# Loading the pages of a paged cache: plain DMAs on the sync queue with the page number in a register, in place of indirect gathers on GpSimd

## The chip, the cores and the metric

The kernel runs on one NeuronCore of a Trainium2 chip. The metric is the time of the whole program on the device in microseconds (us): 1012.88 us is the median of three runs of the kernel before (1011.87 to 1016.22). A change below about 0.5% (5 us) can't be told from no change with this kernel. Engines are named as in the profile: PE (TensorE's matmuls), PEld (its weight loads), DVE (VectorE), ACT (ScalarE), POOL (GpSimd) and SP (SyncE, which here only issues DMAs).

## The reference: what is computed

One layer of a hybrid decoder for two groups that share all weights: a prompt of 512 positions and 8 samples with one new position each. Per layer:

```
x += W_out [ GatedDeltaNet heads (8 x 64) | NSA heads (8 x 64) ]( RMSNorm(x) @ W_in )
x += MemCrossAttn( RMSNorm(x), mem K/V )      (4 heads x 256, 256 memory tokens)
x += relu( RMSNorm(x) @ W_up )^2 @ W_down
```

and a final RMSNorm. The prompt has no past. Each sample has a past of 256 positions, which lies in a paged cache: `page_table[b, 0..1]` holds the numbers of two pages of 128 positions, out of 20 pages in all. For every sample the pages of its past are used three times: their compressed keys (`cmp_k`) and compressed values (`cmp_v`) go through a small MLP, and their selected keys and values (`slc_k`, `slc_v`) are attended to directly. So 16 pages are loaded four times, each time another 64 KB quarter of the page (128 rows of 512 bytes): 64 loads in all.

```
kv_all = jnp.concatenate([kv_past, kv_rows], axis=1)          # kv_past = pages[page_table]
k_cmp = compress_blocks(kv_all[:, :, 0], cmp_pe[0], cmp_w1[0], cmp_b1[0], cmp_w2[0])
v_cmp = compress_blocks(kv_all[:, :, 1], cmp_pe[1], cmp_w1[1], cmp_b1[1], cmp_w2[1])
```

## The kernel before

All activations are kept with features on the partitions. A weight panel of 128 output columns (`wraw`, 512 KB) is loaded by SP, split by ACT and DVE into a high and a low part (`whi`, `wlo`; `split`, L235 and L236), and multiplied in three matmuls for each of 8 pieces of the contraction (`mm3`, L194 by way of `mm`) with the two halves of the positions, 256 and 264 wide. The two buffers of `wraw` and of `whi`/`wlo` set how early a panel can be loaded.

`mixers` is the part that the change touches. It runs first a fixed sequence: the panels of the gates and of k0, k1, q0, q1 of the delta rule, the compressed keys `ck` (L500 stands behind it), then the panels k2, k3, q2, q3 with the compression MLP of the keys between them (`cmp_hidden(0)`). Behind that, `weave` lets five generators take turns by an estimate of the time on PE: `rule` (the delta rule: solve, then the chain over four chunks, `dn_chain`, whose step L888 to L928 needs the state of the step before), `nsa_samples`, `nsa_prompt` (the attention of the prompt), `fill` (the remaining panels of W_in and then `mem_kv`, the 16 panels `w_mk` and `w_mv` of the memory's keys and values, as filler for PE) and `mixed`. On top of this the framework orders the instructions of every engine with a simulated timeline (`TILE = dict(schedule_with_timeline_sim=True)`); so the order on each engine, and where a DMA stands in its queue, is decided there, not by the order of the source alone. Each queue works in that order: a DMA whose wait isn't met holds up all that stand behind it on the same queue.

Pages are loaded by `gather` (L517 to L520). It is called from two places. `cmp_gather(kind)` (L535) loads 16 quarters of pages into the tile G, for the keys (kind 0) after `ck`, for the values (kind 1) when the MLP of the keys has read G; G lies in the space of the tile x, so that the first burst waits for the last reader of x, an ACT square (L396). `nsa_samples` (L1273, L1276) loads the selected keys into the space of the tile qk0 and the selected values into the first half of the tile P; both belong to the delta rule and come free piece by piece when the matmuls of `dn_mats` and of the chain have read them. Before the change each of the 64 loads is an indirect DMA on POOL's queue, which takes its 128 row numbers from the tile `idx`, worked out by one DVE instruction from the page table:

```
self.nc.gpsimd.indirect_dma_start(
    out=out, out_offset=None, in_=self.I["pages"],
    in_offset=bass.IndirectOffsetOnAxis(ap=self.idx[:, k:k + 1], axis=0), element_offset=off)
```

In the profile these are `DMA_INDIRECT` instructions of L518. `cAQ` (L932) is a load of the chain's matrix from DRAM on SP's queue; it has one buffer, so that a load waits until PE has read the one before.

Of the kernel before, what the change touches and what calls it, by code (L numbers as in the profile page):

```python
# [10 lines left out]
I32 = mybir.dt.int32  # L11
AF = mybir.ActivationFunctionType
ALU = mybir.AluOpType
# [13 lines left out]
C_ID, C_TRI, C_UP, C_BLK, C_I64, C_CMPM, C_CMPA, C_HB, C_OWN, C_PP, C_CAU = (  # L27
    0, 128, 256, 384, 512, 576, 608, 640, 648, 664, 665)
# [153 lines left out]
class Build:  # L182
# [325 lines left out]
    def load_pages(self):  # L508
        nc, I, mp = self.nc, self.I, self.mp
        pg = mp.tile([128, 16], I32, name="pg")  # L510
        nc.sync.dma_start(pg[:], I["page_table"])
        self.idx = mp.tile([128, 16], I32, name="idx")
        nc.vector.tensor_scalar(self.idx[:], pg[:], 128.0, self.cst[:, C_PP:C_PP + 1], op0=ALU.mult, op1=ALU.add)
        self.w2 = mp.tile([128, 2, 64], F32, name="w2")
        nc.sync.dma_start(self.w2[:], I["w2"])

    def gather(self, out, k, off):  # L517
        self.nc.gpsimd.indirect_dma_start(  # L518
            out=out, out_offset=None, in_=self.I["pages"],
            in_offset=bass.IndirectOffsetOnAxis(ap=self.idx[:, k:k + 1], axis=0), element_offset=off)  # L520


    def cmp_tile(self, kind, h, ps):
# [1304 lines left out]
```

## Time and profile before

| what | before |
|---|---|
| median of 3 runs | 1012.88 us (1011.87 to 1016.22) |
| the profiled execution's own time | 1010.35 us |
| its span, first to last instruction | 1008.6 us |
| mean granted clock of PE | 0.98 |
| busy: PE, DVE, ACT, POOL | 953.5, 693.5, 483.8, 212.8 us |
| indirect DMAs on POOL (L518): into G, qk0, P | 32, 16, 16: 35.9, 17.5, 15.3 us busy |
| DMA moved | 123.78 MB, mean 123 GB/s |

The profile is of one execution. A row of the groups gives the line, the engine, the operation, what it writes and reads, how often, then its busy time and the mean of one in ns, then the idle time of the engine just before it and what ended that. `SPq` rows are SP's queue: the time beside them is that from the first to the last issue of the merged row, not of the transfer. In the chain of waits, "another core or an unknown queue" is a wait whose release the profile can't put down to an instruction, and "issue" is time in which the engine waited for nothing that the profile shows.

### The profile page before, as it was taken

To read this page: it belongs to the slowest core of one execution; us is meant where nothing else is said; L and a number is where in the kernel's file an instruction comes from. 1 tells how busy PE (TensorE), PEld (TensorE's weight loads), DVE (VectorE), ACT (ScalarE), POOL (GpSimd) and SP (SyncE) were. 2 spreads that over 40 slices of the span, in tenths; PEclk is the share of its full clock that TensorE was granted. 3 is DMA by queue.
4 is the path that set the end of the run, shared out by engine and by line. 5 is a ranking of instruction groups with operands and counts; after the bars stand their busy time and mean duration, and the time that the engine had idled before them with its cause. 6 is when DMAs were issued, how large, how long until landed. Compare 5 with 4: busy or idle time off the path is not lost.

```text
span 1008.6 us, 20477 instructions
## 1 busy us (share of the span) xinstructions
PE 953.5 (95%) x8160; PEld 877.5 (87%) x8160; DVE 693.5 (69%) x1406; ACT 483.8 (48%) x1041; POOL 212.8 (21%) x273
## 2 busy tenths in 40 slices
PE   6999798999968999999999999999999999999995
PEld 5988597798856886679998889999999999999995
DVE  6788349898734877865656558799766676666533
ACT  4675213158633635535444446567445544445331
POOL 2634615813074315202400002200000000000020
PEclk9999799999988999999999999999999999999998
DMA  7355243212011464344636634023323232323302
GB/s 272 115 176 162 96 143 126 72 67 75 24 40 51 146 221 178 133 173 157 251 141 240 228 129 161 2 84 126 109 92 105 95 105 85 116 84 108 123 12 85
DMA packets 49832, 123.78 MB, mean 123 GB/s; under 512 B 7608, under 2 KB 15480, under 8 KB 47016
## 3 DMA queue, kind: packets, MB, share of 16 engines
q1 hardware_dynamic: 45480, 109.10, 31.0%
q0 software_dynamic: 4256, 13.37, 3.7%
q8 instruction: 64, 1.05, 0.4%
q14 instruction: 32, 0.26, 0.1%
HBM read 111.06 MB, written 13.47 MB: 123 GB/s over the span
## 4 chain that ended last, share of the span: by engine, by line
PE 83%; DVE 9%; issue 2%; another core or an unknown queue 2%; DMA 1%; ACT 1%; POOL 0%; DVEq 0%; SPq 0%; ACTq 0%; POOLq 0%
PE ps_g L194 37%; PE ps_o L194 14%; PE ps_m L194 11%; PE ps_t L194 10%; PE ps_s L194 8%; PE ps_t L226 2%; DVE wlo L236 1%; PE ps_m L226 1%; DVE nb L806 1%; DVE x L1625 1%; DVE kp L1159 1%; DVE st L821 1%; DMA cAQ<-aqd 1%; DVE Xd L823 0%
## 5 line engine op out<-in xcount | busy, mean ns | idle before, releaser
L194 PE MATMUL ps_g<-xh,whi 128*128 128x264 f32 (+1 forms) x672 | 196.2, 293 | 3.4 <-ACT xh L235 1.1
L194 PE MATMUL ps_g<-xl,whi 128*128 128x264 f32 (+1 forms) x672 | 194.4, 290 | 2.4 <-DVE xl L236 1.5
L194 PE MATMUL ps_g<-xh,wlo 128*128 128x264 f32 (+1 forms) x672 | 193.2, 288 | 1.9 <-DVE wlo L236 1.5
L301 POOL TENSOR_TENSOR ssq<-ssq,sq 128x256 f32<-128x256 f32 (+2 forms) x47 | 44.4, 945 | 514.5 <-ACT sq L300 514.2
L194 PEld LDWEIGHTS ps_g<-xh,whi 128*128 128x128 f32 x672 | 128.9, 192 | 8.7 <-issue 4.3
L194 PEld LDWEIGHTS ps_g<-xh,wlo 128*128 128x128 f32 x672 | 128.5, 191 | 5.3 <-issue 2.7
L194 PEld LDWEIGHTS ps_g<-xl,whi 128*128 128x128 f32 x672 | 129.0, 192 | 3.8 <-DVE xl L236 1.6
L235 ACT CAST whi<-wraw 128x1024 fp32r<-128x1024 f32 (+1 forms) x67 | 69.6, 1040 | 103.1 <-PE ps_g L194 62.0
L235 ACT CAST wh<-wr 128x512 fp32r<-128x512 f32 x112 | 69.1, 623 | 66.7 <-PE ps_g L194 27.6
L236 DVE TENSOR_TENSOR wlo<-wraw,whi 128x1024 fp32r<-128x1024 f32 (+1 forms) x67 | 83.1, 1240 | 23.7 <-ACT whi L235 23.0
L236 DVE TENSOR_TENSOR wl<-wr,wh 128x512 fp32r<-128x512 f32 x112 | 76.4, 687 | 28.8 <-ACT wh L235 26.8
L194 PE MATMUL ps_g<-tyh,wl 128*128 128x260 f32 x256 | 72.3, 283 | 1.1 <-DVE wl L236 1.1
L194 PE MATMUL ps_g<-tyh,wh 128*128 128x260 f32 x256 | 72.6, 284 | 0.0
L194 PE MATMUL ps_g<-tyl,wh 128*128 128x260 f32 x256 | 72.5, 283 | 0.0
L194 PE MATMUL ps_o<-hh,wh 128*128 128x260 f32 x256 | 72.4, 283 | 0.0
L194 PE MATMUL ps_t<-hh,wh 128*128 128x260 f32 x256 | 72.4, 283 | 0.0
L194 PE MATMUL ps_t<-hh,wl 128*128 128x260 f32 x256 | 72.3, 283 | 0.0
L194 PE MATMUL ps_o<-hh,wl 128*128 128x260 f32 x256 | 72.3, 283 | 0.0
L194 PE MATMUL ps_o<-hl,wh 128*128 128x260 f32 x256 | 72.2, 282 | 0.0
L194 PE MATMUL ps_t<-hl,wh 128*128 128x260 f32 x256 | 72.1, 282 | 0.0
L235 ACT CAST wh<-ws 128x512 fp32r<-128x512 f32 x64 | 39.6, 619 | 48.0 <-PE ps_o L194 32.4
L236 DVE TENSOR_TENSOR wl<-ws,wh 128x512 fp32r<-128x512 f32 x64 | 43.8, 685 | 18.7 <-ACT wh L235 18.6
(470 smaller groups left out, 2616.3 us busy)
## 6 DMA issues: line engine op xcount, KB each, us to landing
wr<-in_w_up SPq DMA_DIRECT2D x64, 256.0 KB, 2.8
wr<-in_w_dn SPq DMA_DIRECT2D x64, 256.0 KB, 2.5
wraw<-in_w_in SPq DMA_DIRECT2D x26, 512.0 KB, 4.5
mK<-in_mkt SPq DMA_DIRECT2D x8, 1024.0 KB
mK<-in_mv SPq DMA_DIRECT2D x8, 1024.0 KB, 5.6
w<-in_w SPq DMA_DIRECT2D x8, 512.0 KB, 4.3
wraw<-in_w_mk SPq DMA_DIRECT2D x8, 512.0 KB, 3.2
wraw<-in_w_mv SPq DMA_DIRECT2D x8, 512.0 KB, 3.2
```

The source lines that it names most:

```text
L194: self.nc.tensor.matmul(out, lhsT, rhs, start=start, stop=stop, skip_group_check=True)
L226: self.nc.tensor.transpose(out, in_, self.ident[:k, :k])
L235: self.nc.scalar.copy(hi, x)
L236: self.nc.vector.tensor_tensor(lo, x, hi.bitcast(F32), op=ALU.subtract)
L301: nc.gpsimd.tensor_tensor(acc[:, :n], acc[:, :n], sq[:, :n], op=ALU.add)
L806: nc.vector.transpose(nb[s], P[s, :, s].rearrange("p c i -> p i c"))
L821: eng.tensor_tensor(tv, nb[:, j + 1:32, j].unsqueeze(2).to_broadcast([128, n, m]), x[:, j - c0, 0:m].unsqueeze(1).to_broadcast([128, n, m] ...
L1159: nc.vector.tensor_tensor(t[rows, 1, :], src, t[64 * g:64 * g + 64, 0, :].bitcast(F32), op=ALU.subtract)
L1625: nc.vector.scalar_tensor_tensor(x[:, i, :], ps, self.gain(4, i), x[:, i, :], op0=ALU.mult, op1=ALU.mult)
```

## The change

`load_pages` reads each of the 16 page numbers from the page table in SBUF into a register of SP, and `gather` becomes a plain DMA of SP's queue whose source begins at row 128 * page of the cache. The row numbers `idx` are no longer worked out. What is loaded, and where to, stays as it was.

```diff
-        self.idx = mp.tile([128, 16], I32, name="idx")
-        nc.vector.tensor_scalar(self.idx[:], pg[:], 128.0, self.cst[:, C_PP:C_PP + 1], op0=ALU.mult, op1=ALU.add)
+
+        n = I["pages"].shape[0] // 128
+        self.page = [nc.values_load(pg[0:1, k:k + 1], engines=[mybir.EngineType.SP], min_val=0, max_val=n - 1,
+                                    skip_runtime_bounds_check_because="entries of the page table are pages of the cache") for k in range(16)]
         self.w2 = mp.tile([128, 2, 64], F32, name="w2")
         nc.sync.dma_start(self.w2[:], I["w2"])
 
     def gather(self, out, k, off):
-        self.nc.gpsimd.indirect_dma_start(
-            out=out, out_offset=None, in_=self.I["pages"],
-            in_offset=bass.IndirectOffsetOnAxis(ap=self.idx[:, k:k + 1], axis=0), element_offset=off)
+        self.nc.sync.dma_start(out, self.I["pages"][bass.ds(self.page[k] * 128, 128), off:off + 128])
```

Since the simulated timeline orders each engine anew, here is where the loads come to stand. First SP's queue early in `mixers`, before the change: `wraw<-in_w_in` are panels of W_in (the fourth of the row `x4` is k2), `w<-in_w` the weights of the compression MLP, `cumd` and `P<-cumd` tables of the delta rule.

```order
L1282 DMA out_win_s<-in_win 8x4x16320
L243 DMA wraw<-in_w_in 128x1024 x4
L554 DMA w_962<-in_w 128x1024
L243 DMA wraw<-in_w_in 128x1024
L689 DMA cumd<-ct 32x128
L765 DMA P<-cumd 128x512 x8
```

and after the change:

```order
L1282 DMA out_win_s<-in_win 8x4x16320
L243 DMA wraw<-in_w_in 128x1024 x3
L514 TENSOR_LOAD pg
L520 ISA
L520 DMA G<-in_pages 128x128
...
L243 DMA wraw<-in_w_in 128x1024
L554 DMA w_1008<-in_w 128x1024
L243 DMA wraw<-in_w_in 128x1024
L689 DMA cumd<-ct 32x128
L765 DMA P<-cumd 128x512 x8
```

The three rows L514, L520, L520 stand there 16 times in a row: a load of a page number into a register, one instruction of register arithmetic, the DMA. All 16 stand ahead of the panel k2. The other 48 page loads have only the last two rows.

On POOL, the second burst into G and the loads into qk0 go, and what is left moves together (a piece of the difference):

```order
 L539 DMA G<-in_pe 128x32
-L518 DMA G<-in_pages,idx 128x128 x16
 L530 DMA out_kvp<-kv 128x520
-L518 DMA qk_214<-in_pages,idx 128x128 x2
 L604 DMA out_kvp<-nks 128x520
-L518 DMA qk_214<-in_pages,idx 128x128 x2
 L604 DMA out_kvp<-nkw 128x520
 L808 MEMSET Xs 128x1024
```

The third place is SP's queue where the chain of the delta rule starts; `wraw<-in_w_mk` are the panels of the memory's keys. Before:

```order
L243 DMA wraw<-in_w_in 128x1024 x12
L1635 DMA xm<-in_xm 128x1024 x2
L932 DMA cAQ<-aqd 128x1024 x2
L243 DMA wraw<-in_w_mk 128x1024 x5
L932 DMA cAQ<-aqd 128x1024
```

and after:

```order
L243 DMA wraw<-in_w_in 128x1024 x12
L1635 DMA xm<-in_xm 128x1024 x2
L932 DMA cAQ<-aqd 128x1024
L243 DMA wraw<-in_w_mk 128x1024
L520 ISA
L520 DMA qk_260<-in_pages 128x128
...
L520 DMA P<-in_pages 128x128
L243 DMA wraw<-in_w_mk 128x1024 x2
...
L932 DMA cAQ<-aqd 128x1024
L243 DMA wraw<-in_w_mk 128x1024 x4
```

The 24 page loads there (8 into qk0, 8 into P, and behind two panels another 8 into P) stand ahead of the second `cAQ`; the first panel of `w_mk` stands ahead of them all, and the second and third ahead of the last eight. Before, all five stood behind the second `cAQ`.

## The prediction

> **What bounds the kernel now.** First the page's busy times, the clock by slices, and the shares of the chain that ended last.
>
> ```profile
> span 1008.6 us, 20477 instructions
> ...
> PE 953.5 (95%) x8160; PEld 877.5 (87%) x8160; DVE 693.5 (69%) x1406; ACT 483.8 (48%) x1041; POOL 212.8 (21%) x273
> ...
> PEclk9999799999988999999999999999999999999998
> ...
> PE 83%; DVE 9%; issue 2%; another core or an unknown queue 2%; DMA 1%; ACT 1%; POOL 0%; DVEq 0%; SPq 0%; ACTq 0%; POOLq 0%
> ```
>
> PE sets the time: it is idle for 55 of 1008.6 us, and POOL, which issues the gathers, has no share in the chain. So the busy time that leaves POOL is worth nothing by itself. What the change can move is PE's 55 idle us, and the slices in which its clock falls (the fifth, the twelfth and the thirteenth of the 40). So I read PE's waits next: engine, line and releaser, then us in total, times, longest.
>
> ```profile
> PE ps_m L194 <- DVE S L928: 5.0, 1, 5.0
> PE ps_m L194 <- DVE kcz L576: 4.7, 1, 4.7
> ```
>
> Two long waits happened once each, behind DVE copies that are short. The timelines of PE and DVE show the first of them (start, duration, what; in brackets the idle time ahead and what ended it).
>
> ```profile
> 282.35 0.69 PE L194 MATMUL ps_m<-cvn,kt 128*64 128x64 f32 x16
> ...
> 289.57 0.80 PE L194 MATMUL ps_m<-S,qk 128*128 128x128 f32 x2 [5.03 <-DVE S L928]
> ```
> ```profile
> 288.64 0.88 DVE L928 COPY S<-ps_m 64x256 f32<-64x256 f32 x2 [5.15 <-remote]
> ```
>
> The copy of S needs only the matmuls on `cvn,kt`, which are recorded as done at 283.04. Yet DVE starts at 288.64, after 5.15 us of waiting for something that no instruction explains, and PE stands still behind it. The news of a finished matmul came over 5 us late. POOL's timeline says what ran meanwhile:
>
> ```profile
> 98.19 1.00 POOL L518 DMA_INDIRECT G<-in_pages,idx  x1 [0.30 <-issue]
> ...
> 117.39 0.94 POOL L518 DMA_INDIRECT G<-in_pages,idx  x1 [0.30 <-issue]
> ```
> ```profile
> 287.56 0.94 POOL L518 DMA_INDIRECT P<-in_pages,idx  x1 [0.30 <-issue]
> ```
>
> The eighth gather into P ends at 288.50, and 0.14 us later DVE is released. The last of the 16 gathers of the second burst ends at 118.33. The unexplained pieces of the chain of waits (start, us) fit both bursts:
>
> ```profile
> 106.61 4.39 another core or an unknown queue
> ...
> 111.45 3.76 another core or an unknown queue
> ...
> 115.93 2.11 another core or an unknown queue
> ```
> ```profile
> 283.49 5.13 another core or an unknown queue
> ...
> 296.69 3.92 another core or an unknown queue
> ```
>
> These five sum to 19.31 us, all between the first and last gather of a dense burst. That the gathers delay PE's signals is my reading of a coincidence in time; no row shows the mechanism. The windows give the size: from:to, length, busy us of PE, PEld, DVE, ACT, POOL, then clock, DMA share, GB/s.
>
> ```profile
> 105.00:125.00 20.00, 13.13 (x68) 9.99 (x66) 6.26 (x16) 4.48 (x8) 12.86 (x14) 0.74 0.22 68
> 250.00:275.00 25.00, 25.00 (x429) 21.39 (x428) 17.87 (x42) 15.85 (x44) 2.53 (x3) 1.00 0.09 31
> 282.00:325.00 43.00, 30.81 (x251) 23.81 (x250) 16.65 (x35) 14.11 (x39) 25.54 (x29) 0.80 0.14 47
> 325.00:350.00 25.00, 25.00 (x264) 20.13 (x263) 21.88 (x44) 16.93 (x45) 8.11 (x9) 1.00 0.45 148
> ```
>
> In the two bursts PE is idle for 6.87 and 12.19 us, at 0.74 and 0.80 of its clock; just before and behind the second it is never idle, at full clock. Bandwidth isn't short: the bursts move 68 and 47 GB/s, the quiet stretch behind 148. The clock is halved only behind each stall, and these windows cover the busy time at half clock:
>
> ```profile
> 119.00:125.00 6.00, 5.14 (x17) 3.81 (x17) 3.02 (x8) 2.42 (x4) 2.58 (x3) 0.51 0.20 61
> 289.00:296.00 7.00, 6.43 (x31) 5.43 (x32) 4.21 (x10) 1.83 (x5) 5.09 (x7) 0.53 0.13 40
> 303.00:306.00 3.00, 3.00 (x17) 2.03 (x16) 1.46 (x4) 1.16 (x3) 0.88 (x2) 0.53 0.06 22
> 316.00:323.00 7.00, 6.20 (x30) 4.70 (x32) 1.53 (x3) 1.60 (x5) 1.72 (x2) 0.51 0.22 84
> ```
>
> Busy time times the missing share of the clock: 5.14 x 0.49 = 2.5, 6.43 x 0.47 = 3.0, 3.00 x 0.47 = 1.4, 6.20 x 0.49 = 3.0; together 9.9 us. (The 0.26 and 0.20 of the whole windows would count idle time twice.)
>
> **The change part by part.** *Removed: the gathers.* Idle 6.87 + 12.19 = 19.1 us, and 9.9 us of half clock, are 29.0 us. The neighbouring windows put the natural idle time near nothing; I leave 1 us of it, so the gain is **28 us**. Bounds: nothing, if the stalls are not the gathers' doing; 29 and a few us more, if the panels issued earlier (below) fill idle time that I counted as natural. I take 28 because start and end of the stalls agree with the bursts to 0.2 us. POOL itself gets rid of 32 + 16 + 16 gathers,
>
> ```profile
> L518 POOL DMA_INDIRECT G<-in_pages,idx x32 | 35.9, 1123 | 9.7 <-issue 9.1 <-DMA G<-in_pages,idx 0.3 <-DVE cum L681 0.3
> ```
>
> some 36 us of busy time for G and, at the same mean, as much for the other 32, all off the path; the DVE instruction for `idx` goes too, a fraction of a us at the start, also off it.
>
> *Added: SP's first burst.* SP now carries 16 times a register load, register arithmetic and a DMA, ahead of panel k2. SP's queue today, the panel's landing, POOL's release of G and ACT's use of k2:
>
> ```profile
> 14.48 22.32 SPq L243 DMA_DIRECT2D wraw<-in_w_in  x4
> ...
> 53.62 4.86 SPq L765 DMA_DIRECT2D P<-cumd  x8
> ```
> ```profile
> wraw<-in_w_in SPq DMA_DIRECT2D x26, 512.0 KB, 4.5
> ```
> ```profile
> 30.10 0.73 POOL L539 DMA_DIRECT2D G<-in_pe  x1 [16.99 <-ACT sq L396]
> ```
> ```profile
> 53.94 1.05 ACT L235 CAST whi<-wraw 128x1024 fp32r<-128x1024 f32 x1 [2.54 <-remote]
> ```
> ```profile
> 59.60 1.07 PE L194 MATMUL ps_o<-G,w 128*128 128x81 f32 x6 [0.17 <-ACT sgm L704]
> ```
>
> Before, k2 is issued by 36.8 (14.48 + 22.32) and ACT takes it at 53.94: 12.6 us of cover after a landing of 4.5. After, the page loads can't start before G is free at 30.1, and k2 waits for all 16. One DMA of SP costs 0.61 us (4.86 / 8). The register load isn't in this trace. From below it is one of the smallest engine steps, 0.17 us; from above a whole small transfer with its landing, 1.9 us:
>
> ```profile
> 32.35 0.17 DVE L721 COPY cv<-pre 128x3 f32<-128x3 f32 x1
> ```
> ```profile
> small<-in_small SPq DMA_DIRECT2D x1, 77.5 KB, 1.9
> ```
>
> A load of four bytes from SBUF is nearer to the former, and I take 0.5 us. One page then costs 1.1 to 1.15 us with the arithmetic, 16 cost 18.4, and SP is free at 48.5; k2 lands at 53.0, just ahead of the cast. At 0.17 it is free at 42.6 and nothing is lost. At 1.9 the 16 cost 16 x 2.51 = 40.2, k2 lands at 74.8, and ACT is 20.9 us late. All of that would be PE's, since ACT's next steps stand behind the cast and PE already waits on one of them (0.17 us at 59.60). I book **2 us** for this place. The Trainium skill, page "DMA: Bandwidth & Descriptors", section "Latency and other measured facts", gives a floor of about 0.6 us for a tensor load. By that figure, as an estimate, 16 would take 19.4 us and k2 would land at 54.0, the same place; no run here shows it.
>
> *Added: the second and third bursts on SP.* They have no register loads. Sixteen DMAs take 16 x 0.61 = 9.8 us from 98 on, against 20.1 us on POOL (98.19 to 118.33). Behind them on SP stand a store of `aqd`, a piece of the MLP's weights, and then the next panel. The first two were issued before at
>
> ```profile
> 111.48 0.33 SPq L795 DMA_DIRECT2D aqd<-AQ  x1
> 123.83 0.33 SPq L554 DMA_DIRECT2D w<-in_w  x1
> ```
>
> both later than 98 + 9.8 = 107.8: no cost. If that cover were gone, the loss would be the overshoot past 123.8.
>
> *Moved: the memory's panels.*
>
> ```profile
> 260.94 57.39 SPq L932 DMA_DIRECT2D cAQ<-aqd  x2
> 326.18 18.76 SPq L243 DMA_DIRECT2D wraw<-in_w_mk  x5
> ```
>
> Before, all five panels wait behind the second `cAQ`, which is issued at 318.3 when PE has read the first. After, the first panel stands ahead of the 24 page loads, and two ahead of the last 8. The page loads wait for PE's last reads of qk0 and P (before: until about 306.3, the last eight after 2.3 us more of idle POOL); eight take 4.9 us, which ends before 318.3, so `cAQ` isn't late. The early panels give PE filler in the very stretch where it stalls; from full coverage of 325 to 350 I book nothing, and keep it for the low end. Each page load also waits for an earlier DMA of the same queue slot to land; with 64 KB each this hides behind the issue pitch.
>
> Sum: -28 + 2 = **-26 us**. The profiled execution took 1010.35 us (span 1008.6 and 1.75 around it), 2.5 below the median of 1012.88. So 984.3 for an execution like it, and 1012.88 - 26 = **987 us** for the median.
>
> **The rivals.** *Register loads hold k2* (faster, but less). For it: k2 has 0 to 1 us to spare by my sum, and the price is the one that no row shows. Against: the nearest small steps are far below 1 us. At 1.2 us a load, 16 x 1.81 = 29.0, k2 lands at 63.6, 9.7 us late: -28 + 9.7 gives 994.6. At 1.9 it is -28 + 20.9, 1005.8.
>
> *No change.* The stalls could belong to something that stays, such as the delta rule's pattern of PE and DVE, with gathers only beside them; or plain DMAs of SP delay the signals as well. For it: the lateness follows the gathers in time only, and in the first burst PE loses next to nothing, though ACT waits 2.54 us for "remote" there (the row at 53.94):
>
> ```profile
> 50.00:62.00 12.00, 11.83 (x85) 10.48 (x84) 8.75 (x24) 8.08 (x14) 7.02 (x13) 1.00 0.67 214
> ```
>
> Against: PE had other work there, and SP's eight issues of `P<-cumd`, every 0.61 us in the same window, stop nothing. Time: 1012.9 less nothing. A rule of the Trainium skill would have it so: page "DMA: Bandwidth & Descriptors", section "Issuing engines are not separate DMA queues", says that issuing from another engine saves only the sequencer's issue time; and POOL's issue time is off the path here. The trace speaks against it, with 19 us of PE's waiting that end when the gathers do.
>
> *SP becomes the bound (slower).* A page load is 128 rows of 512 bytes at an address in a register, and its pitch X on SP is unknown. Behind the first burst k2 is late by 30.1 + 16 X + 4.5 - 53.9 = 16 X - 19.3; behind the second the MLP's weights by 98 + 16 X - 123.8 = 16 X - 25.8. Both exceed the 28 saved from X = 2.3, and the bound for slower from 2.45. At X = 3 the losses are 28.7 and 22.2, net +22.9: 1035.8. For it: 64 KB in 512-byte rows has no like on SP. Against: SP's issues so far take 0.33 to 0.9 us whatever their shape.
>
> **How the numbers follow.** My forecast 0.70, register loads 0.14, no change 0.06, SP as the bound 0.10. What this kernel's measurement can tell from no change is about 0.5%, 5 us: the first two are faster by more, so 0.84, same 0.06, slower 0.10. The range: low 974, which is the whole 29.0 us without the 2 us of cost, and some 10 us that earlier panels and freed POOL and DVE may give; high 1007, the register load at its upper bound. The cases outside hold 0.16.
>
> **What would show it right or wrong.** Right: the chain's "another core or an unknown queue" falls from 19 us in these stretches to under 3; windows 105:125 and 282:325, shifted to the same work, have PE above 95% busy and a clock above 0.97; no DVE or ACT row there waits for "remote" over 2 us. The step on k2: ACT's cast of it starts near 53 and waits less than 2 us on `wraw`; a wait of 10 or 20 us there is the first rival, and the pitch of the 16 triples on SP prices it. If "remote" waits stand beside SP's bursts instead, the no-change rival is right. What makes 987 wrong with the mechanism right is the half clock: should PE's clock fall behind some new short wait, up to 10 us come back.

## The result, and the profile after

| | before | after |
|---|---|---|
| median | 1013.09 us (1011.87 to 1016.22, 4 runs) | 980.85 us (979.04 to 983.10, 4 runs) |
| the profiled execution's own time, its span | 1010.35, 1008.6 us | 981.79, 979.9 us |
| PE busy, idle in the span | 953.5, 55 us | 945.0, 35 us |
| mean granted clock of PE | 0.98 | 0.991 |

The ratio is 0.9679, with a 95% interval of 0.966 to 0.9697: 3.2% faster. The medians stand 32 us apart, the two profiled executions 28.6. The forecast was 987 us, 26 less than before. The other 3.7 us between the medians' difference and the profiles' come from which executions were profiled: before's lay 2.7 us under its median, after's 0.9 over.

From the page of the changed kernel, the busy times, the clock by slices and the shares of the chain:

```profile
PE 945.0 (96%) x8160; PEld 870.5 (89%) x8160; DVE 695.0 (71%) x1405; ACT 481.4 (49%) x1041; POOL 144.3 (15%) x209
...
PEclk9999999999999999999999999999999999999997
...
PE 84%; DVE 10%; DMA 2%; ACT 2%; issue 1%; SPq 0%; POOL 0%; DVEq 0%; ACTq 0%
```

"Another core or an unknown queue" is gone from the chain, and the three slices with a low clock are gone too. Of the 28.7 us of span, 20 are idle time of PE and 8.5 busy time. The windows of the changed kernel, with the columns of the prediction's, show the place of the first burst (25 to 75), the work of before's 105 to 125 us (94 to 114, as it runs up to 11 us earlier now), the start of the chain (what stood at 283 stands at 273.6 now), and 282 to 325:

```profile
25.00:50.00 25.00, 25.00 (x198) 23.95 (x196) 17.12 (x46) 12.96 (x29) 3.97 (x9) 1.00 0.36 119
50.00:75.00 25.00, 25.00 (x176) 22.23 (x176) 23.62 (x69) 20.37 (x36) 0.82 (x3) 1.00 0.50 162
94.00:114.00 20.00, 20.00 (x137) 17.09 (x138) 14.67 (x40) 9.77 (x17) 1.92 (x4) 1.00 0.58 179
...
272.00:300.00 28.00, 26.72 (x284) 22.39 (x285) 23.11 (x39) 17.34 (x42) 9.74 (x13) 1.00 0.52 167
...
282.00:325.00 43.00, 43.00 (x461) 36.06 (x459) 32.14 (x60) 22.36 (x59) 6.55 (x9) 1.00 0.41 136
```

PE is idle in these for 1.28 us (272 to 300) and otherwise never, at full clock; before, it was idle for 6.87 and 12.19 us in the second burst and in the chain. Not all of that was waiting for DVE or ACT. Two rows of before's waits in these windows (105 to 125, then 282 to 325) are PE standing still with nothing to wait for that the profile shows:

```profile
PE ps_g L194 <- issue: 1.8, 3, 0.8
```
```profile
PE ps_m L194 <- issue: 4.5, 8, 1.1
```

The eight of the second row lie between 310.9 and 317.6 us, where the last eight gathers into P run (306.28 to 315.98). They are gone after the change too. The same instructions in both timelines show where the span became shorter:

| instruction | before, us | after, us | difference |
|---|---|---|---|
| DVE L328, third `kv` | 105.28 | 104.41 | -0.9 |
| DVE L1290, `few` | 123.72 | 112.55 | -11.2 |
| ACT L1201, last `np` ahead of the stall at 283 | 283.19 | 273.56 | -9.6 |
| DVE L926, fifth `S` | 369.21 | 343.41 | -25.8 |
| ACT L235, a panel of the next stage | 489.21 | 460.02 | -29.2 |
| end of the span | 1008.6 | 979.9 | -28.7 |

About 10 us come in the second burst into G and 16 in the chain of the delta rule, where the prediction put them, and 3.4 between the chain and the next stage, where it booked nothing. What the prediction could not know came out when the kernel before was run on other chips.

### The profile page after: what moved, and what is told of

It is laid out like the page before. It is cut to its first block, busy times and chain, and to the rows that moved or that the text cites. A ratio compares the mean times of both kernels' runs of the same rounds, so it can differ in the third digit from the quotient of the medians.

```text
span 979.9 us, 20589 instructions
## 1 busy us (share of the span) xinstructions
PE 945.0 (96%) x8160; PEld 870.5 (89%) x8160; DVE 695.0 (71%) x1405; ACT 481.4 (49%) x1041; POOL 144.3 (15%) x209
## 4 chain that ended last, share of the span: by engine, by line
PE 84%; DVE 10%; DMA 2%; ACT 2%; issue 1%; SPq 0%; POOL 0%; DVEq 0%; ACTq 0%
PE ps_g L194 37%; PE ps_o L194 14%; PE ps_m L194 11%; PE ps_t L194 11%; PE ps_s L194 8%; PE ps_t L226 2%; DVE wlo L236 1%; DMA wraw<-in_w_in 1%; DVE nb L806 1%; DMA out_mk_o<-mk 1%; PE ps_m L226 1%; DVE st L821 1%; DVE Xd L823 1%; DVE x L1625 1%; DVE kp L1159 1%
## 5 line engine op out<-in xcount | busy, mean ns | idle before, releaser
L235 ACT CAST whi<-wraw 128x1024 fp32r<-128x1024 f32 (+1 forms) x67 | 69.4, 1037 | 95.0 <-PE ps_g L194 47.6
L235 ACT CAST wh<-wr 128x512 fp32r<-128x512 f32 x112 | 68.9, 620 | 67.4 <-PE ps_g L194 28.2
L236 DVE TENSOR_TENSOR wl<-wr,wh 128x512 fp32r<-128x512 f32 x112 | 76.3, 687 | 28.7 <-ACT wh L235 26.8
L235 ACT CAST wh<-ws 128x512 fp32r<-128x512 f32 x64 | 39.5, 617 | 48.7 <-PE ps_o L194 32.5
```

Source lines behind the costliest of these rows:

```text
L235: self.nc.scalar.copy(hi, x)
L236: self.nc.vector.tensor_tensor(lo, x, hi.bitcast(F32), op=ALU.subtract)
```

## The experiments

The runs were made on four chips, each time with the kernel before beside them. I name the chips in the order of their appearance: A (runs 1 to 4), B (5 to 7, and 11), C (8 to 10), D (12). Which chip the first comparison ran on isn't recorded.

**Run 1: plain DMAs, but on POOL.** `values_load` puts the page numbers into registers of POOL (pieces of the difference to the changed kernel, as in the diffs that follow):

```diff
-engines=[mybir.EngineType.SP]
+engines=[mybir.EngineType.Pool]
-        self.nc.sync.dma_start(out, self.I["pages"][bass.ds(self.page[k] * 128, 128), off:off + 128])
+        self.nc.gpsimd.dma_start(out, self.I["pages"][bass.ds(self.page[k] * 128, 128), off:off + 128])
```

> The 64 loads go back to POOL's queue, as plain DMAs whose page number stands in a register of POOL; only the list of row numbers is gone. Theory A (the indirect form is what delays PE's signals): no stalls, 980 to 987 us. Theory B (any dense burst on POOL's queue does it): the stalls stay, PE idle about 7 and 12 us in the two stretches, 1005 to 1013 us. Theory C (the gain is POOL's freed time): POOL stays busy with as many issues, so 1005 us or more, but without late signals.

**Runs 2 and 3: one part of the change alone.** The loads into G on SP, the others indirect on POOL, and the other way round; the row numbers `idx` are worked out again for the indirect ones:

```diff
     def gather(self, out, k, off):
+        if off < 256:              # run 3: off >= 256
             self.nc.sync.dma_start(out, self.I["pages"][bass.ds(self.page[k] * 128, 128), off:off + 128])
+        else:
+            self.nc.gpsimd.indirect_dma_start(...)
```

> Only the 32 loads into G go to SP; the 32 into qk0 and P stay indirect gathers of POOL. In the traces the second burst is worth 11 us and the last stretch 17. Theory A and B: 1013 - 11 = 1002 us (998 to 1006), with the stall at 282 to 325 still there. Theory C: half of POOL's time is freed, half of the gain, 997 us.

> Only the 32 loads into qk0 and P go to SP; the 32 into G stay indirect gathers of POOL. Theory A and B: 1013 - 17 = 996 us (992 to 1000), the stall behind the second burst into G still there, about 7 us of idle PE. Theory C: 997 us, but without a stall in particular there.

**Run 4: gathers that nobody reads, added to the changed kernel.**

```diff
+        late = mp.tile([128, 1], F32, name="late")
+        nc.vector.scalar_tensor_tensor(late[:], vvs[0][0][:, 0, 0, 0:1], 0.0, self.cst[:, C_PP:C_PP + 1], op0=ALU.mult, op1=ALU.add)
+        idx = mp.tile([128, 16], I32, name="idx")
+        nc.vector.tensor_scalar(idx[:], self.pg[:], 128.0, late[:], op0=ALU.mult, op1=ALU.add)
+        for k in range(16):
+            nc.gpsimd.indirect_dma_start(out=self.unread[:, k, :], ..., element_offset=384)
```

> The changed kernel, and beside it 16 indirect gathers on POOL that nobody reads: 128 rows of 32 bytes each into a spare tile, released when the first selected values have landed, where the chain of the delta rule begins. Theory A and B: PE's signals are late there again, about 10 us lost: 988 to 997 us. Theory C: POOL has time to spare, 980 to 984 us. If the bytes did it, a sixteenth of them would do next to nothing: 981 to 983.

Measured on chip A:

| kernel | median, us | ratio to the kernel before (95%) |
|---|---|---|
| before | 985.45 (22 runs) | |
| 1, plain on POOL | 976.55 | 0.9904 (0.9880 to 0.9927) |
| 2, only G on SP | 981.69 | 0.9988 (0.9957 to 1.0018) |
| 3, only qk0 and P on SP | 985.35 | 0.9992 (0.9967 to 1.0017) |
| 4, 16 unread gathers | 989.15 | 1.0037 (1.0016 to 1.0058) |

The first line upset all three theories: the kernel before, unchanged, took 28 us less than in the first comparison. None of the expectations of runs 1 to 3 holds as a number, since these were reckoned from 1013. Run 4's 989.15 lies in the range of theories A and B (988 to 997), but by luck, as its windows show. Run 2 has single times from 978 to 991, and its interval leaves open whether it is faster at all. Run 4's group on POOL and its windows, around its dense burst (284 to 305 us) and behind it:

```profile
L1284 POOL DMA_INDIRECT unread<-in_pages,idx x16 | 16.0, 1003 | 6.6 <-issue 4.3 <-DVE idx L1282 2.0 <-DMA unread<-in_pages,idx 0.3
```
```profile
275.00:300.00 25.00, 23.73 (x251) 19.82 (x252) 21.50 (x40) 14.87 (x38) 17.24 (x19) 1.00 0.65 192
300.00:325.00 25.00, 25.00 (x267) 21.53 (x264) 16.50 (x29) 11.37 (x27) 8.78 (x9) 1.00 0.33 106
...
375.00:400.00 25.00, 20.54 (x158) 13.57 (x150) 24.82 (x46) 13.23 (x35) 12.96 (x11) 0.86 0.36 136
```

The gathers run, and PE loses 1.3 us in the 50 around them. The kernel is slower, but 70 us later, where its work is ordered in another way; I didn't follow that further. On this chip these dense indirect gathers came without the stall. Was it the chip, or had I misread the profile?

**Runs 5 and 6: both kernels once more, unchanged.**

> The kernel before, unchanged, with a profile of its own. In the first four experiments' company it took 985.45 us, 28 less than the 1013.09 of the first comparison, and the three of them with dense indirect gathers on POOL show no late signal of PE. Theory D (whether dense gathers delay PE's signals depends on the chip or its condition): either 985 us, with gathers as dense as ever, no unexplained wait in the chain and PE over 95% busy at 105 to 125 and 282 to 325, or 1013 us with the stalls. Theory E (the stalls are always there, and the 28 us lie elsewhere): 985 us with the stalls still to be seen.

> The changed kernel, unchanged, beside the kernel before on the same chip. Theory D: where the stalls are absent the change is worth only what remains, 977 to 983 us against 985 (0 to 8 us); where they are there, 981 against 1013 again. Theory E: 950 to 960 us against 985.

**Run 7: no register loads.** Pages 0 to 15 as constants; the look-up in the page table and the `values_load` lines are left out:

```diff
-        self.nc.sync.dma_start(out, self.I["pages"][bass.ds(self.page[k] * 128, 128), off:off + 128])
+        self.nc.sync.dma_start(out, self.I["pages"][128 * k:128 * k + 128, off:off + 128])
```

> The changed kernel with pages 0 to 15 as constants in place of the page table: no register loads and no register arithmetic on SP; it leaves out the look-up, so it computes with other pages. In the changed kernel the 16 loads of the first burst stand 0.9 us apart on SP, and panel k2 came to ACT 2.9 us late, while PE stayed 100% busy. My theory: the 16 take 9 to 10 us, ACT's wait for k2 goes, the time stays within 2 us of the changed kernel. Rival (the delay of k2 does reach PE later): 2 to 4 us faster than the changed kernel.

Measured on chip B, where the kernel before took 986.53 us (25 runs): run 5, the same kernel, 987.16 (0.9996, 0.9969 to 1.0023); run 6, the changed kernel, 980.60 (0.9937, 0.9910 to 0.9963); run 7 981.20 (0.9951, 0.9926 to 0.9975). POOL's timeline of run 5, first and last gather of the second burst, and its windows:

```profile
102.36 1.00 POOL L518 DMA_INDIRECT G<-in_pages,idx  x1 [0.30 <-issue]
...
121.87 0.95 POOL L518 DMA_INDIRECT G<-in_pages,idx  x1 [0.30 <-issue]
```
```profile
105.00:125.00 20.00, 20.00 (x144) 17.25 (x143) 11.88 (x34) 6.90 (x12) 15.34 (x16) 1.00 0.39 130
282.00:325.00 43.00, 39.65 (x391) 30.75 (x393) 30.31 (x58) 26.31 (x69) 29.81 (x32) 0.92 0.35 106
```

It is the very kernel and the same burst, 16 gathers in 20.5 us. In the first profile PE was idle for 6.87 of these 20 us, here not at all; at 282 to 325 it is idle for 3.35 us instead of 12.19. No wait in its chain is left to an unknown queue. Theory D holds: whether PE stalls beside dense indirect gathers depends on the chip or its condition. On chip B the change is worth about 6 us, not 32.

Where do these 6 us come from? Run 5's PE timeline shows a wait that the first profile doesn't have, with the windows around it, and the tile view of G (time from issue to landing of the gathers up to 66 us):

```profile
62.49 1.06 PE L194 MATMUL ps_o<-G,w 128*128 128x81 f32 x6 [2.17 <-DMA P<-cumd]
```
```profile
59.00:63.00 4.00, 1.83 (x15) 1.65 (x15) 3.99 (x15) 3.18 (x6) 0.12 (x1) 1.00 1.03 392
63.00:70.00 7.00, 7.00 (x39) 6.14 (x39) 6.48 (x24) 3.90 (x7) 2.85 (x6) 0.76 0.52 181
```
```profile
DMA to landing us min/median/max: 2.5/3.4/6.9
```

The first burst on POOL ends at 56.5 us. By then SP has issued most of the eight loads of `P<-cumd`, 256 KB each; the DMA engines are full (share 1.03, 392 GB/s), and one gather takes 6.9 us to land, against a median of 3.4. PE waits 2.17 us for the first product with G (the row puts the end of the wait down to `P<-cumd`, in flight beside the gathers; run 8 below names the gather), and 7 us at 0.76 of its clock behind it cost another 1.7. Run 7 prices the register loads; SP's timeline of run 7 and of run 6, the changed kernel on the same chip:

```profile
29.19 7.71 SPq L517 DMA_DIRECT2D G<-in_pages  x16
36.99 0.38 SPq L243 DMA_DIRECT2D wraw<-in_w_in  x1
```
```profile
29.85 13.48 SPq L520 DMA_DIRECT2D G<-in_pages  x16
43.42 0.38 SPq L243 DMA_DIRECT2D wraw<-in_w_in  x1
```

From the first issue to the last there are 15 steps, 7.27 us in run 7 and 13.14 in run 6. So a page load alone takes 0.48 us of SP, with register load and arithmetic 0.88: the register costs 0.40. The profile of run 6 gives a register load about 0.27 us of that, the first 0.50:

```profile
L514 SPq TENSOR_LOAD <-pg x16: 262/270/496, 28.9 to 42.5; - x16
```

The panel k2 is issued 6.4 us earlier without them, and the time doesn't change.

**Runs 8 to 10: the first burst.** Run 8 is the changed kernel with the first burst as indirect gathers of POOL again (`off > 0` as the condition for SP), run 9 the changed kernel, run 10 the kernel of run 1.

> The changed kernel with only the first burst (16 loads into G for the keys) as indirect gathers on POOL again. In two profiles whose first burst is on POOL, PE waits 2.2 us at the first product with G, its clock halves behind that, and the last gather took 6.5 and 6.9 us to land beside the eight loads of P<-cumd. Theory F (what the change is worth where PE's signals are in time is this landing): slower than the changed kernel by 3 to 5 us, so 984 to 986 us against 981, PE idle about 2 us at 59 to 63 us. Rival G (the gain is spread over the later order of work): within 1.5 us of the changed kernel. If the chip shows PE's signals late as in the first profile, the kernel before takes 1013 us, and this kernel, without the dense bursts behind 90 us, still 985 or less.

> The changed kernel, unchanged, as the measure for the other two. 980 to 982 us; 0.5 to 1% faster than the kernel before where that takes 986 us, 3% where it takes 1013.

> Plain DMAs of POOL with the page number in a register of POOL, as in the first experiment, now beside the changed kernel on one chip. The issues take about 0.55 us each on POOL against 1.1 for an indirect gather, G's first burst is done by 45.5 us, before P<-cumd starts, and SP's queue holds nothing back. 976 to 978 us, 3 to 5 us faster than the changed kernel; the rival that the first measurement was a matter of the chip gives no difference within 1.5 us. On a chip with late signals: theory A (only the indirect form delays them) 977 again, theory B (any dense burst of POOL's queue) 1000 or more.

Measured on chip C, before at 985.87 us (24 runs): run 8 986.89 (1.0008, 0.9985 to 1.0031), run 9 981.39 (0.9961, 0.9936 to 0.9986), run 10 977.23 (0.9914, 0.9883 to 0.9944). Run 8's PE timeline and landing times, and run 9's landing times:

```profile
60.98 1.06 PE L194 MATMUL ps_o<-G,w 128*128 128x81 f32 x6 [2.26 <-DMA G<-in_pages,idx]
```
```profile
DMA to landing us min/median/max: 2.5/3.1/6.3
```
```profile
DMA to landing us min/median/max: 1.8/1.9/3.0
```

Putting 16 of the 64 loads back costs 5.5 us, a little more than expected, and so takes the whole gain away. The wait names the gather itself now, 2.26 us, with one landing at 6.3 us. With the loads on SP, issued by 44 us, none takes longer than 3.0. So on this chip the gain needs the first burst, as theory F has it. Run 10 is 4.2 us faster than the changed kernel on one chip (976.1 to 980.7 against 977.7 to 985.1), so it beats both.

**Run 11: the counterpart,** only the first burst on SP (`off == 0`).

> The counterpart of the eighth run: only the first burst (16 loads into G for the keys) goes to SP, the other 48 stay dense indirect gathers of POOL. Theory F: where PE's signals are in time this one burst is the whole worth of the change, 980 to 983 us against 986, no wait of PE at the first product with G. Rival G (spread over the later order): 984 to 986. If the chip shows PE's signals late, the stalls at 105 to 125 and 282 to 325 us are there in its profile and it takes 1005 us or more, as the kernel before would (1013).

On chip B again, before at 986.25 us (17 runs): 983.07, ratio 0.9979 (0.9956 to 1.0002). Its window at that place:

```profile
59.00:63.00 4.00, 4.00 (x28) 3.52 (x27) 4.00 (x16) 3.91 (x8) 0.00 (x0) 1.00 0.88 298
```

The wait at the first product with G is gone, as it should be, but the median falls by 3.2 us rather than by 5, and the interval just reaches no change. So the first burst is needed for the gain; by the medians, that it is all of it isn't shown. The profiles say where it comes and that little is left. One instruction behind the first burst, and the end of the span, in us:

| run (chip) | first burst | DVE, third `kv` | end of the span |
|---|---|---|---|
| 5, before (B) | indirect | 108.73 | 988.1 |
| 8 (C) | indirect | 107.31 | 983.4 |
| 6, changed (B) | SP | 103.45 | 978.7 |
| 9, changed (C) | SP | 103.86 | 978.8 |
| 11 (B) | SP | 103.14 | 979.7 |

With the burst indirect, 3.5 to 5.6 us are lost by the third `kv`. In its one profiled execution run 11 ends 1 us behind the changed kernel. It keeps a second place where gathers are waited for, in the chain: PE is idle for 3.27 us at 282 to 325 in run 11 (3.35 in run 5, none in runs 6 and 9), and the chain of waits runs there through the gathers into qk0 and their landing:

```profile
286.81 4.35 DMA qk<-in_pages,idx
```

What that place is worth wasn't measured apart.

**Run 12: G by plain DMAs of POOL, qk0 and P by SP.**

```diff
-engines=[mybir.EngineType.SP]
+engines=[mybir.EngineType.Pool, mybir.EngineType.SP]
+        queue = self.nc.gpsimd if off < 256 else self.nc.sync
-        self.nc.sync.dma_start(out, self.I["pages"][bass.ds(self.page[k] * 128, 128), off:off + 128])
+        queue.dma_start(out, self.I["pages"][bass.ds(self.page[k] * 128, 128), off:off + 128])
```

> Plain DMAs with the page number in a register throughout: the 32 loads into G on POOL's queue, the 32 into qk0 and P on SP's. It asks where the 4 us lie by which the version wholly on POOL is faster than the changed kernel. If in the early part (SP free for panel k2, which then isn't 2.9 us late at ACT): 976 to 978 us. If in the chain of the delta rule (the second cAQ and the w_mk panels without 24 page loads ahead of them on SP): 980 to 982 us. PE has no wait over 1 us at the first product with G in either case. On a chip with late signals (before 1013) it would say whether plain dense bursts of POOL bring them: a wait of 4 us or more for nothing known between 98 and 112 us.

On chip D the kernel before took 1013.86 us (9 runs, 1010.46 to 1015.49): by its time, the condition of the first comparison was back. The kernel before has no profile on D, so that its 28 us lie in the same stalls isn't shown. Run 12 took 980.60, ratio 0.9681 (0.9659 to 0.9702). POOL's timeline of run 12 at the second burst, and its windows:

```profile
96.71 6.55 POOL L521 DMA_DIRECT2D G<-in_pages  x11
```
```profile
85.00:110.00 25.00, 25.00 (x171) 21.27 (x170) 18.50 (x46) 13.32 (x23) 11.68 (x22) 1.00 0.53 162
105.00:125.00 20.00, 20.00 (x152) 17.72 (x151) 9.49 (x28) 4.57 (x8) 2.54 (x5) 1.00 0.40 131
282.00:325.00 43.00, 43.00 (x449) 36.48 (x448) 29.78 (x57) 21.12 (x55) 5.12 (x6) 0.96 0.40 130
```

Eleven plain DMAs of POOL in 6.55 us are twice as dense as the gathers were, on a chip where the kernel before loses its 28 us, and PE is never idle. That speaks against theory B, POOL's queue in itself, for the bursts into G, and for theory A, the indirect form. It doesn't settle it: all 16 plain loads of that burst are over in 9.9 us (96.71 to 106.57), half the time of the gathers, and in the first profile the first unexplained wait began 8.4 us into the burst. As to its own question, run 12 sits with the changed kernel (980.6 and 980.85 where before is 1013) rather than with run 10, so the 4 us of run 10 seem to lie in the chain. The profiles of runs 9 and 10, both on chip C, agree: the third `S` of DVE's L926 (L925 in run 10) starts at 317.84 and 318.12 us, the fifth at 342.64 and 339.83. By then SP's page loads in run 9 are over (292.2), so nothing stands behind them in SP's queue at that moment; which difference in the order of work gives the 4 us stays open.

## Why the prediction was right or wrong

*The stalls.* Right on a chip like the first one. The sum was 29.0 us, of which 28 were booked; the two stretches gave about 10 + 16, and lost all but 1.3 us of their idle time and the half clock. The two signs named beforehand came out: no unexplained piece is left in the chain, and no wait for "remote" over 2 us. That the measured difference of the profiled executions, 28.6, is so near to the 28 booked is in part luck: 26.5 lie in the two stretches, and 3.4 come behind them, for which nothing was booked.

*The reading of the mechanism.* Half right. The prediction called it a coincidence in time that no row explains, and gave 0.06 to the stalls being something else. The same kernel with the same bursts takes 985 to 987 us on chips A, B and C (88 runs), and its profile on B has no such stalls. So the gathers are not enough; in the first comparison something else has to be there, and on D too if its loss is the same one. That the gathers are needed there rests on the changed kernel and run 12, neither of which has a burst of them, and on the timing in the first profile; both kernels also have another order of work, so this is argued and not shown. Late signals are not the whole of it either: 6.3 of the 19.1 us of idle PE are waits of its own with no releaser. And since the profile models the ends of matmuls, it can't tell a late signal from a product that was finished late. Which condition of the chip it is stays open. A version on D with fewer or thinner gathers wasn't tried. The step that failed is an unspoken one: that a stall seen in one profile belongs to the kernel, wherever it runs. On B and C the forecast would have been wrong as a size (about 0.5% faster instead of 2.6%), though the 981 us measured there lie in its range. That the comparison was made where the stalls occur was luck.

*The cost on SP ahead of k2.* The 2 us booked were not lost, and the reasoning had three errors. The register load, taken as 0.5 us, costs 0.40 with its arithmetic, less than the 0.6 that the prediction quotes for the load alone, and a page load 0.48 rather than 0.61, so 16 took 13.6 us instead of 18.4. Next, k2 was matched with the wrong cast. ACT's timeline before, then after:

```profile
45.51 1.05 ACT L235 CAST whi<-wraw 128x1024 fp32r<-128x1024 f32 x1 [1.19 <-PE ps_g L194]
```
```profile
48.22 1.05 ACT L235 CAST whi<-wraw 128x1024 fp32r<-128x1024 f32 x1 [2.94 <-DMA wraw<-in_w_in]
...
53.90 1.05 ACT L235 CAST whi<-wraw 128x1024 fp32r<-128x1024 f32 x1 [0.15 <-DMA wraw<-in_w_in]
```

The cast that reads k2 is the one at 45.51, not the one at 53.94; the cover was 45.5 - 41.3 = 4.2 us, not 12.6. ACT did wait 2.94 us for it, more than the 2 that the prediction named as its sign. And "all of that would be PE's" was wrong: PE is busy for all of the 25 us from 25 to 50 in the changed kernel (windows above), as it was before, and run 7, with k2 6.4 us earlier, is no faster.

*What the prediction missed.* The last gathers of the first burst land late beside `P<-cumd`, and PE waits for them. In the first profile this doesn't show (0.17 us of wait there, for ACT; it has no landing times of the gathers). In runs 5 and 8 it costs 2.2 us of waiting and the clock behind it, and 3.5 to 5.6 us by the third `kv`. The prediction looked only at what the loads do to SP's queue, not at when the old gathers landed.

*The rivals.* Register loads holding k2: the wait came, but it cost nothing that run 7 could show. No change: not on the first chip; on B and C the gain is 4 to 6 us, near the bound of what can be told. SP as the bound: a page load of 128 rows takes 0.48 us of SP, 0.88 with its register load, not the 2.3 to 3 that this rival needed. The rule quoted from the Trainium skill ("DMA: Bandwidth & Descriptors", section "Issuing engines are not separate DMA queues") would have given no gain. On B and C the gain is 4 to 6 us, since the last gathers were late for PE. In the first comparison and on D it is 32 and 33 us. There the change took another form of DMA as well as another queue; where only the queue differs, in runs 9 and 10, the times are 4.2 us apart, with another order of work.

## What to carry to other kernels

A stall that the profile can't put down to an instruction may belong to the chip that the profile came from, as the 1013 us here against 986 elsewhere show: before building on it, run the unchanged kernel on another chip. Removing indirect gathers was still the safe choice, since plain DMAs with the page number in a register for all loads took 977 to 982 us on every chip seen, while the gathers took 986 or 1013. And it paid here to issue a burst of small loads before large ones filled the DMA engines: the last landing took 3.0 us instead of 6.3 to 6.9, and the last landing is what the consumer waited for.

## What the runs showed that I had not expected

- The same kernel took 985 to 987 us on three chips and 1013 to 1014 on a fourth and in the first comparison, each within about 0.6% on its chip. In the one profile of the slower case the difference is idle time and half clock of PE beside dense indirect gathers.
- A register load with its arithmetic lengthens a stream of SP's DMAs by 0.40 us per DMA (0.48 to 0.88).
- A plain DMA of POOL for the same 64 KB takes 0.55 us of POOL, against 1.1 for the indirect gather. This group of run 1 answers to the prediction's of 32 gathers into G (35.9 us):

```profile
L520 POOL DMA_DIRECT2D G<-in_pages x32 | 17.9, 558 | 8.4 <-issue 5.8 <-DMA G<-in_pages 1.2 <-DVE be L667 0.4
```
